# Half of the up projection with seven products, and 29 weight remainders by an adding DMA

## The chip, the cores and the metric

The kernel runs on one core of a Trainium2 chip. The metric is the device time of one execution in microseconds. Matrix products run on TensorE (PE in the profile), elementwise work on VectorE (DVE) and ScalarE (ACT); GpSimd (POOL) and SyncE (SP) mostly issue DMAs here.

## The reference

One layer of an encoder on 256 tokens of width 2048: a retention branch and an attention branch are merged by gates, then comes the MLP, which the change is in. All is float32.

```python
def reference(x, ...):
    h = x
    for l in range(DEPTH):                                # DEPTH = 1
        u = _rmsnorm(h, norm_mix_g[l])
        h = h + _mixer(u, positions, ...)                 # both branches
        z = _rmsnorm(h, norm_mlp_g[l]) @ w_up[l]          # 256x2048 @ 2048x8192
        h = h + jnp.square(jax.nn.relu(z)) @ w_down[l]    # 256x8192 @ 8192x2048
    return _rmsnorm(h, norm_f_g)
```

## The kernel before

**Three products for one.** A float32 operand is split into two parts of the format fp32r: `hi` is a cast of the value, `lo` the remainder value minus `hi`. A product of two operands is then hi·hi + hi·lo + lo·hi. The helper `split` (L548) does it: `SC.copy(hi, val)` on ScalarE, then a subtraction on VectorE. Every weight is loaded as a `raw` tile by a DMA of SP and split before it is used.

**The up projection has two forms.** Of the 64 column tiles of 128, the first `ST` = 24 (`SU` = 3 blocks of 1024 columns) go by seven products instead of eight (class `Step`), and the other 40 go one by one (class `Unit`).

- A `Unit` (L1219) has two parts, one for each half of the 2048 rows of weights. A part loads 512 KB, splits them, and multiplies: `t_pass1` (L176) has eight products of `w.hi` with 512 columns, in which both parts of the tokens lie side by side, `t_pass2` (L180) eight of `w.lo` with 256 columns. Pass 1 needs `hi` alone, pass 2 needs `lo`. After part 1, `evict` copies the bank to `hs` on ScalarE (L1246) and adds its halves on VectorE (L1247). Two iterations later (`later`, `soon`) come relu, square and the store to `hid` in HBM by a DMA of POOL (L1250, L1211, L1212).
- A `Step` has four parts and takes two row tiles of a block, and eight steps (`SJ`) make a block. It forms sums of the weights (L307, L316, L317, on VectorE), splits its seven operands in parts of 2, 2, 2 and 1, and issues 21 products of 512 columns (L333 to L335) with token sums that were made beforehand (`hc`). At a block's end `s_end` (L515) copies four banks on ScalarE and adds on VectorE (L520), and in the next steps four turns (`turn`, L1257) transpose the result on TensorE (L1264), followed by relu, square and store.

**The order is written out by hand.** The list `parts` holds the parts of all units and steps, and behind them those of the down projection. `stream` (L470) goes through it, and all engines keep the order in which it writes their instructions:

```python
for n, (it, h) in enumerate(parts):
    ahead = AHEAD if n else 2                        # AHEAD = 4
    while loaded < min(len(parts), n + ahead + 3): ...   # load of part n+6
    while prepped < min(len(parts), n + ahead + 1): ...  # prep of part n+4
    it.mm(h)                                         # products, and a unit's evict
    after(n)
    soon(n)
```

In ScalarE's queue the preparation of part n+4 thus stands ahead of what `mm` of part n appends, the copy of `evict` among it, and the preparation of part n+5 stands behind it. Tiles come in rings: five for `raw`, and seven pairs for `hi` and `lo`, four of them under these names and three under `morehi` and `morelo`; a pair is free again when TensorE is done with the part seven places before.

**Where the units stand.** The first three units (`EARLY`) go ahead of the steps, the last two (`LATE`) behind them; the turns of the last block are spread over these two. The other 35 stand behind the last part (h = 3) of all 23 steps but the last one, and twelve of them behind the second part (h = 1) of a step.

Of the kernel before, what the change touches and what calls it, by code (L numbers as in the profile page):

```python
# [16 lines left out]
AF = mybir.ActivationFunctionType  # L17
ALU = mybir.AluOpType
# [9 lines left out]
CHUNK = 64  # L28
DFF = 8192
FT = DFF // P  # L30
SU = 3
SJ = KT // 2
ST = SU * 1024 // P
EARLY, LATE = 3, 2
AHEAD = 4
PAIRED = 6
MAKE = 7, 2 * EARLY + 18
SUMS = (4, 7, 10), (0, 1, 2)
MANUAL = {getattr(mybir.EngineType, n) for n in ('Activation', 'DVE', 'PE', 'SP', 'Pool')}
# [66 lines left out]
def block_kernel(ctx: ExitStack, tc: tile.TileContext, A):  # L106
    nc = tc.nc
    V, SC, G, PE = nc.vector, nc.scalar, nc.gpsimd, nc.tensor
# [7 lines left out]
    def big(name, dt=F32, shape=(P, KT, S)):  # L116
        return act.tile(list(shape), dt, tag="act16", name=name)

    class Pair:
        def __init__(self, name):  # L120
            self.t = [big(f"{name}{i}", F32R, (P, KT // 2, 2, S)) for i in range(2)]
# [35 lines left out]
    def wtile(kind, shape):  # L157
        uid[0] += 1
        dt, bufs = (F32, 5) if kind == "raw" else (F32R, 4)
        return wp.tile(shape, dt, tag=kind, bufs=bufs, name=f"{kind}{uid[0]}")  # L160
# [11 lines left out]
    HK = KT // 2  # L172
# [100 lines left out]
    def pair(shape):  # L273
        pool, more = env["pool"], env["more"]
        slot[0] += 1
        if slot[0] % (4 + more) < 4:
            return [wtile(kind, shape) for kind in ("hi", "lo")]
        if env["big"]:
            t = env["big"][:, slot[0] % (4 + more) - 4]
            n = math.prod(shape[1:])  # L280
            return [t[:, i, :n].rearrange("p (a b) -> p a b", a=shape[1]) for i in range(2)]
        return [
            pool.tile(shape, F32R, tag=f"more{kind}", bufs=more, name=f"more{kind}{uid[0]}_{slot[0]}")
            for kind in ("hi", "lo")
        ]

    class Step:
# [17 lines left out]
        def prep(self, part):  # L305
            if part == 0:
                V.tensor_tensor(  # L307
                    out=self.fa, in0=self.rb[:, 1:].to_broadcast([P, 2, 512]), in1=self.ra, op=ALU.add
                )
                self.middle()  # L310
            r = (self.ra, self.fa, self.fb, self.rb[:, :1])[part]
            hi, lo = pair([P, r.shape[1], 512])
            split(hi, lo, r)
            self.ws[part] = hi, lo
            if part == 0:
                V.tensor_tensor(out=self.fb[:, 0], in0=self.fa[:, 0], in1=self.ra[:, 1], op=ALU.add)  # L316
                V.tensor_tensor(out=self.fb[:, 1], in0=self.fb[:, 0], in1=self.rb[:, 0], op=ALU.add)  # L317
# [230 lines left out]
    def split(hi, lo, val, scale=None):  # L548
        if scale is None:
            SC.copy(hi, val)  # L550
            V.tensor_tensor(out=lo, in0=val, in1=hi.bitcast(F32), op=ALU.subtract)  # L551
        else:
            SC.activation(hi, val, AF.Copy, scale=scale)
            V.scalar_tensor_tensor(
                lo, in0=val, scalar=scale, in1=hi.bitcast(F32), op0=ALU.mult, op1=ALU.subtract
            )
# [44 lines left out]
    for k in range(KT):  # L601
        t = lead0[:, N_VEC:] if k == 0 else wtile("raw", [P, LEAD])
# [13 lines left out]
        hi, lo = (wtile(kind, [P, FIRSTS * P]) for kind in ("hi", "lo"))  # L616
# [35 lines left out]
    early = ip.tile([P, FIRSTS, S], F32, name="early")  # L652
# [564 lines left out]
        store(pair, 0, t)  # L1217

    class Unit:  # L1219
        def __init__(self, i, order, between=None):  # L1220
            self.i, self.order, self.between, self.raw, self.ws = i, order, between, {}, {}

        def load(self, part):
            self.raw[part] = wtile("raw", [P, HK, P])
# [1 line left out]

        def prep(self, part):
            hi, lo = pair([P, HK, P])
            split(hi, lo, self.raw.pop(part))
            self.ws[part] = hi, lo  # L1230

        def mm(self, part):
# [24 lines left out]
    def turn(u, jj):  # L1257
        pT = atps(f"zt{u}{jj}")
        for j in range(2):
            kt = 2 * jj + j  # L1260
            for t in range(2):
                o = j * S + t * P
                src = zo[:, 0, 2 * t + kt // 4, kt % 4 * P : kt % 4 * P + P]
                PE.transpose(pT[:, o : o + P], src, ident)  # L1264
        square(4 * u + jj, pT)

    def step(u, j, qs):
        def end():
            sums = s_end(qs, zo[:, 0].rearrange("p (t c) n -> p t c n", t=2), zo[:, 1])
            next(sums)  # L1270
            later.extend([d, lambda: next(sums)] for d in SUMS[u == SU - 1])
            turns.extend(lambda jj=jj: turn(u, jj) for jj in range(4))

        def between():
            if turns and j:
                turns.pop(0)()

        return Step(qs, A["w_up_s"][u, j], hc, j, between, end)

    def drain(n):  # L1280
        def fn(part):
            for _ in range(n[part]):
                turns.pop(0)()
        return fn

    early = [Unit(i, 0) for i in range(EARLY)]
    parts = [(e, h) for h in range(2) for e in early]
    units = list(range(EARLY, FT - ST - LATE))
    slots = [(u, j, h) for u in range(SU) for j in range(SJ) for h in (1, 3)][:-1]
    whole = [t for t in slots if t[2] == 3]  # L1290
    room = len(units) - len(whole)
    halves = [t for t in slots if t[2] == 1]
    if room >= 0:
        use = set(whole) | {halves[i * len(halves) // room] for i in range(room)}
    else:
        use = {t for t in whole if t[1] != PAIRED or t[0] >= -room}
    for u in range(SU):
        qs = {}
        for j in range(SJ):
            st = step(u, j, qs)  # L1300
            for h in range(4):
                parts.append((st, h))
                if (u, j, h) in use:
                    un = Unit(units.pop(0), 0)
                    parts += [(un, 0), (un, 1)]
    assert not units
    for n, i in enumerate(range(FT - ST - LATE, FT - ST)):
        un = Unit(i, 0, drain(((0, 1), (1, 2))[n]))
        parts += [(un, 0), (un, 1)]

    hp = ctx.enter_context(tc.tile_pool(name="hp", bufs=1))
# [57 lines left out]
    def finish(half, t, c, n, lo=0, hi=512):  # L1369
        h = residual(half, t, c)[:, lo:hi]  # L1370
        ps = both[half].q[ROLE[t, c]][:, lo:hi]
        V.scalar_tensor_tensor(h, in0=ps, scalar=rh2[:, t : t + 1], in1=h, op0=ALU.mult, op1=ALU.add)

        def square():
            SC.activation(ps, h, AF.Square, accum_out=ssf[:, t, n : n + 1])

        return square
# [31 lines left out]
    order = [*range(ST // 2, DP), *range(ST // 2)]  # L1409
# [58 lines left out]
    with tc.manual_schedule(engines=MANUAL):  # L1468
        stream(parts, after)
        assert not later  # L1470
        for t in range(2):
            for c in range(2):
# [10 lines left out]
                else:  # L1483
                    halves = [finish(1, t, 1, 3, 0, 256)]
# [86 lines left out]
```

## Time and profile before

| | before |
|---|---|
| time, median of 3 runs | 1578.91 us (1578.73 to 1579.29) |
| profiled execution, first to last instruction (span) | 1577.3 us |
| what lies around the span, median less span | 1.6 us |
| granted TensorE clock, mean | 0.998 |
| busy PE, DVE, ACT, POOL | 1565.2, 1313.6, 959.0, 38.9 us |
| DMA, read from HBM and written to it | 319.72 MB, 12.58 MB |
| up stage | from about 889 to 1236 us of the span |
| down stage | from about 1236 to 1570 us |

The profile gives one execution's span and no time of its own beside it; the span and the median of the runs differ by 1.6 us. Busy times are sums over the instructions of an engine. A matrix product of 512 columns has a duration of about 0.39 us but starts about 0.23 us after the one before, since products overlap; costs on TensorE are therefore read from the starts in the chain of waits, not from the durations.

### The profile page before, as it was taken

To read this page: it belongs to the slowest core of one execution; us is meant where nothing else is said; L and a number is where in the kernel's file an instruction comes from. 1 tells how busy PE (TensorE), PEld (TensorE's weight loads), DVE (VectorE), ACT (ScalarE), POOL (GpSimd) and SP (SyncE) were. 2 spreads that over 40 slices of the span, in tenths; PEclk is the share of its full clock that TensorE was granted. 3 is DMA by queue.
4 is the path that set the end of the run, shared out by engine and by line. 5 is a ranking of instruction groups with operands and counts; after the bars stand their busy time and mean duration, and the time that the engine had idled before them with its cause. 6 is when DMAs were issued, how large, how long until landed. Compare 5 with 4: busy or idle time off the path is not lost.

```text
span 1577.3 us, 21401 instructions
## 1 busy us (share of the span) xinstructions
PE 1565.2 (99%) x7671; PEld 1317.0 (84%) x7671; DVE 1313.6 (83%) x1780; ACT 959.0 (61%) x1405; POOL 38.9 (2%) x75
## 2 busy tenths in 40 slices
PE   9999999999999999999999999999999999999997
PEld 7888888888898888888888888888888888888886
DVE  7898877899967988875667689887978899989996
ACT  6545655566545667765445566676766766666664
POOL 0000000000000000000000000010000100000000
PEclk9999999999999999999999999999999999999999
DMA  8666655466656564443565666667675977786873
GB/s 322 212 197 205 231 164 161 157 203 208 204 178 222 190 203 142 136 135 132 188 214 186 240 221 226 218 209 236 203 246 196 366 267 244 241 308 216 267 254 114
DMA packets 107626, 333.70 MB, mean 212 GB/s; under 512 B 11264, under 2 KB 12160, under 8 KB 106496
## 3 DMA queue, kind: packets, MB, share of 16 engines
q1 hardware_dynamic: 104208, 318.71, 60.5%
q0 software_dynamic: 3168, 11.54, 1.8%
q10 hardware_dynamic: 144, 2.10, 0.4%
q8 instruction: 60, 0.98, 0.3%
q14 instruction: 46, 0.38, 0.1%
HBM read 319.72 MB, written 12.58 MB: 211 GB/s over the span
## 4 chain that ended last, share of the span: by engine, by line
PE 81%; issue 0%; DVE 0%; ACT 0%; DVEq 0%; POOLq 0%; POOL 0%; ACTq 0%
PE z L176 9%; PE dn L357 7%; PE dn L359 7%; PE dn L358 7%; PE z L180 5%; PE zs L333 2%; PE zs L334 2%; PE zs L335 2%; PE lt L199 2%; PE mo L214 2%; PE mo L217 2%; PE mo L215 2%; PE wo L214 2%; PE wo L215 2%; PE wo L217 2%; PE gm L357 2%
## 5 line engine op out<-in xcount | busy, mean ns | idle before, releaser
L169 DVE TENSOR_TENSOR lo<-raw,hi 128x1024 fp32r<-128x1024 f32 (+1 forms) x148 | 173.2, 1172 | 97.2 <-ACT hi L168 97.0
L551 DVE TENSOR_TENSOR lo<-raw,hi 128x1024 fp32r<-128x1024 f32 (+3 forms) x214 | 232.3, 1102 | 22.9 <-ACT hi L550 22.5
L168 ACT CAST hi<-raw 128x1024 fp32r<-128x1024 f32 (+1 forms) x148 | 149.4, 1011 | 166.2 <-PE mo L215 46.2
L550 ACT CAST hi<-raw 128x1024 fp32r<-128x1024 f32 (+3 forms) x214 | 200.1, 954 | 55.5 <-issue 7.8
L551 DVE TENSOR_TENSOR morelo<-raw,morehi 128x1024 fp32r<-128x1024 f32 (+1 forms) x118 | 127.2, 1099 | 19.6 <-ACT morehi L550 19.1
L550 ACT CAST morehi<-raw 128x1024 fp32r<-128x1024 f32 (+1 forms) x118 | 109.1, 950 | 12.6 <-DMA raw<-w_down 3.9
L550 ACT CAST hi<-forms 128x1024 fp32r<-128x1024 f32 x70 | 73.7, 1053 | 51.7 <-DVE forms L307 28.6
L176 PE MATMUL z<-hT,morehi 128*128 128x512 f32 x408 | 101.6, 391 | 0.0
L357 PE MATMUL dn<-hi,dd 128*128 128x512 f32 x230 | 89.7, 390 | 0.0
L359 PE MATMUL dn<-hi,dd 128*128 128x512 f32 x230 | 89.6, 390 | 0.0
L358 PE MATMUL dn<-lo,dd 128*128 128x512 f32 x230 | 89.6, 389 | 0.0
L551 DVE TENSOR_TENSOR lo<-forms,hi 128x1024 fp32r<-128x1024 f32 x70 | 85.0, 1221 | 5.3 <-ACT hi L550 4.9
L176 PEld LDWEIGHTS z<-hT,morehi 128*128 128x128 f32 x408 | 74.9, 188 | 14.4
L1246 ACT COPY hs<-z 128x512 f32<-128x512 f32 x40 | 23.5, 586 | 71.1 <-PE z L180 71.1
L358 PE MATMUL dn<-morelo,dd 128*128 128x512 f32 x156 | 60.8, 390 | 0.0
L357 PE MATMUL dn<-morehi,dd 128*128 128x512 f32 x156 | 60.8, 389 | 0.0
L359 PE MATMUL dn<-morehi,dd 128*128 128x512 f32 x156 | 60.8, 389 | 0.0
L180 PEld LDWEIGHTS z<-hT,morelo 128*128 128x128 f32 x408 | 55.7, 191 | 4.0
L176 PE MATMUL z<-hT,hi 128*128 128x512 f32 x232 | 57.9, 392 | 0.0
L307 DVE TENSOR_TENSOR forms<-raw,sraw 128x1024 f32<-128x1024 f32 x46 | 56.1, 1220 | 1.0 <-DMA raw<-w_up_s 1.0
L180 PE MATMUL z<-hT,morelo 128*128 128x256 f32 x408 | 56.9, 283 | 0.0
L214 PE MATMUL mo<-hi,my 128*128 128x512 f32 x128 | 50.8, 400 | 0.0
(498 smaller groups left out, 4193.8 us busy)
## 6 DMA issues: line engine op xcount, KB each, us to landing
raw<-w_down SPq DMA_DIRECT2D x106, 512.0 KB, 6.1
raw<-w_up SPq DMA_DIRECT2D x80, 512.0 KB, 5.1
raw<-w_rv SPq DMA_DIRECT2D x32, 512.0 KB, 4.8
raw<-w_rg SPq DMA_DIRECT2D x32, 512.0 KB, 4.2
raw<-w_gret SPq DMA_DIRECT2D x32, 512.0 KB, 4.6
raw<-w_ret_o SPq DMA_DIRECT2D x32, 512.0 KB, 5.1
raw<-w_gmla SPq DMA_DIRECT2D x32, 512.0 KB, 4.6
raw<-w_mla_o SPq DMA_DIRECT2D x32, 512.0 KB, 3.7
```

The costliest lines, as they stand in the source:

```text
L168: SC.copy(hi, raw)
L169: V.tensor_tensor(out=lo, in0=raw, in1=hi.bitcast(F32), op=ALU.subtract)
L176: PE.matmul(out, w[0][:, k], x.both(k0 + k), start=start and k == 0, stop=False)
L180: PE.matmul(out[:, :S], w[1][:, k], x.hi(k0 + k), start=False, stop=stop and k == n - 1)
L214: PE.matmul(out, x.hi(k0 + k, ts), w[0][:, k], start=start and k == 0, stop=False)
L215: PE.matmul(out, x.lo(k0 + k, ts), w[0][:, k], start=False, stop=False)
L217: PE.matmul(out, x.hi(k0 + k, ts), w[1][:, k], start=False, stop=stop and k == nk - 1)
L357: PE.matmul(q, ah, wh, start=start, stop=False)
L358: PE.matmul(q, ah, wl, start=False, stop=False)
L359: PE.matmul(q, al, wh, start=False, stop=self.left[f] == 0)
L550: SC.copy(hi, val)
L551: V.tensor_tensor(out=lo, in0=val, in1=hi.bitcast(F32), op=ALU.subtract)
```

## The change

`SU` goes from 3 to 4. Half of the columns of the up projection now go by seven products, and 32 units are left instead of 40: three early, 27 between the steps, two late.

The 27 units stand behind whole steps alone: there are 31 such places (the last step's is left out), and `use` spreads the units over them evenly, so that four places stay empty. `PAIRED` and the places in the middle of a step are gone.

All units but the three early ones (27 + 2 = 29) get `added=True`. In part 0 of such a unit the remainder is not subtracted on VectorE. ScalarE casts the weights to `hi` as before and casts them once more with the scale -1 into `lo`, which then holds -hi; then POOL issues a DMA that reads the same 512 KB of weights from HBM again and adds them to `lo`. Part 1 of the unit, the early units and the steps are split as before.

```diff
-SU = 3
+SU = 4
...
-PAIRED = 6
...
     class Unit:
-        def __init__(self, i, order, between=None):
-            self.i, self.order, self.between, self.raw, self.ws = i, order, between, {}, {}
+        def __init__(self, i, added=True, between=None):
+            self.i, self.added, self.between, self.raw, self.ws = i, added, between, {}, {}
...
         def prep(self, part):
             hi, lo = pair([P, HK, P])
-            split(hi, lo, self.raw.pop(part))
+            raw = self.raw.pop(part)
+            if part == 0 and self.added:
+                SC.copy(hi, raw)
+                SC.activation(lo, raw, AF.Copy, scale=-1.0)
+                G.dma_start(lo, A["w_up"][self.i][:, part * HK : (part + 1) * HK], accum_op=ALU.add)
+            else:
+                split(hi, lo, raw)
             self.ws[part] = hi, lo
...
-    early = [Unit(i, 0) for i in range(EARLY)]
+    early = [Unit(i, False) for i in range(EARLY)]
     parts = [(e, h) for h in range(2) for e in early]
     units = list(range(EARLY, FT - ST - LATE))
-    slots = [(u, j, h) for u in range(SU) for j in range(SJ) for h in (1, 3)][:-1]
-    whole = [t for t in slots if t[2] == 3]
-    room = len(units) - len(whole)
-    halves = [t for t in slots if t[2] == 1]
-    if room >= 0:
-        use = set(whole) | {halves[i * len(halves) // room] for i in range(room)}
-    else:
-        use = {t for t in whole if t[1] != PAIRED or t[0] >= -room}
+    whole = [(u, j, 3) for u in range(SU) for j in range(SJ)][:-1]
+    use = {whole[i * len(whole) // len(units)] for i in range(len(units))}
...
                 if (u, j, h) in use:
-                    un = Unit(units.pop(0), 0)
+                    un = Unit(units.pop(0))
                     parts += [(un, 0), (un, 1)]
...
-        un = Unit(i, 0, drain(((0, 1), (1, 2))[n]))
+        un = Unit(i, True, drain(((0, 1), (1, 2))[n]))
         parts += [(un, 0), (un, 1)]
```

## The prediction

> **What bounds the kernel now.** I read the chain that ended last first, then the up stage alone (from 889 to 1236 us of the span) in the windows, then who waits for whom inside it.
>
> ```profile
> PE 81%; issue 0%; DVE 0%; ACT 0%; DVEq 0%; POOLq 0%; POOL 0%; ACTq 0%
> ```
>
> ```profile
> core 0: us, PE busy (x) PEld busy (x) DVE busy (x) ACT busy (x) POOL busy (x), PEclk, DMA share, GB/s
> 889.00:1236.00 347.00, 346.99 (x1852) 299.11 (x1851) 292.53 (x335) 237.22 (x340) 26.10 (x48) 1.00 0.67 225
> ```
>
> ```profile
> ACT hs L1246 <- PE z L180: 71.1, 38, 3.6
> ...
> PEld zs L335 <- DVE lo L551: 0.4, 1, 0.4
> ```
>
> The chain is made of matrix products. In the up stage TensorE (PE) is busy 346.99 of 347.00 us at a granted clock of 1.00, VectorE (DVE) 292.53, ScalarE (ACT) 237.22. TensorE waited for a weight once, for 0.4 us. ScalarE waited 71.1 us in 38 places, always in the same one: the copy that empties a unit's bank stands in ScalarE's queue and holds it until the unit's last product is done. So in this stage a product less is time less, as long as every remainder `lo` is there when TensorE asks for it, and the wait in ScalarE's queue decides how early ScalarE can begin with the next one.
>
> **What seven products save.** The chain, in order of time, shows a unit and a step side by side.
>
> ```profile
> 1078.44 1.81 PE z L176 x8
> 1080.25 0.95 PE z L180 x8
> 1081.20 1.84 PE z L176 x8
> 1083.05 0.95 PE z L180 x8
> 1084.00 0.23 PE zs L333
> ...
> 1088.79 1.81 PE z L176 x8
> ```
>
> ```profile
> L1264 PE MATMUL zt<-con,zo 128*128 128x128 f32 x48 | 7.0, 272 | 0.0
> ```
>
> A unit of 128 columns takes 1.81 + 0.95 + 1.84 + 0.95 = 5.55 us, a step of 21 products 88.79 - 84.00 = 4.79 us. The change takes out eight units (44.4 us) and puts in eight steps (38.3 us) and four turns of four transposes each (16/48 of 7.0 us, 2.3 us). TensorE's work falls by 44.4 - 40.6 = 3.8 us. That is all there is to win: 0.24% of the time.
>
> **What it costs VectorE and ScalarE.** The groups of the up stage give the prices.
>
> ```profile
> L551 DVE TENSOR_TENSOR lo<-forms,hi 128x1024 fp32r<-128x1024 f32 x48 | 58.1, 1221 | 4.9 <-ACT hi L550 4.9
> L307 DVE TENSOR_TENSOR forms<-raw,sraw 128x1024 f32<-128x1024 f32 x24 | 29.3, 1219 | 1.0 <-DMA raw<-w_up_s 1.0
> L1247 DVE TENSOR_TENSOR hs<-hs 128x256 f32<-128x256 f32 x40 | 17.0, 424 | 27.6 <-ACT hs L1246 26.6
> L317 DVE TENSOR_TENSOR forms<-forms,raw 128x512 f32<-128x512 f32 x24 | 16.6, 692 | 0.8
> L316 DVE TENSOR_TENSOR forms<-forms,sraw 128x512 f32<-128x512 f32 x24 | 16.5, 686 | 0.0
> L520 DVE TENSOR_TENSOR zo<-zo 128x512 f32<-128x512 f32 x12 | 8.1, 684 | 0.0
> L520 DVE TENSOR_TENSOR zo<-zs,zo 128x512 f32<-128x512 f32 x9 | 6.2, 688 | 0.2
> ```
>
> ```profile
> L550 ACT CAST hi<-forms 128x1024 fp32r<-128x1024 f32 x48 | 50.5, 1053 | 26.1 <-DVE forms L307 18.3 <-DVE forms L317 7.8
> L1246 ACT COPY hs<-z 128x512 f32<-128x512 f32 x40 | 23.5, 586 | 71.1 <-PE z L180 71.1
> L1211 ACT ACTIVATE hs<-hs 128x256 f32<-128x256 f32 (+1 forms) x49 | 22.9, 467 | 1.6
> L1250 ACT ACTIVATE hs<-hs 128x256 f32<-128x256 f32 x38 | 15.6, 411 | 4.8 <-DVE hs L1247 4.7
> L1216 ACT ACTIVATE hs<-zt 128x512 f32<-128x512 f32 x12 | 7.2, 597 | 0.5 <-PE zt L1264 0.5
> L522 ACT COPY zo<-zs 128x512 f32<-128x512 f32 x3 | 1.7, 575 | 0.0
> ```
>
> VectorE: a step is one form of 1.22, two of 0.69, three remainders of 1.22 and one of half that size, for which I take the 0.69 of the other half-size operations, 6.95 us in all; eight are 55.6, and the sums at the end of a block are a third of 8.1 + 6.2, 4.8. Out go eight units with two remainders of 1.2 and one addition of 0.42 each (22.6), and 29 remainders (34.8). The balance is +3.0 us: 295 us of work beside some 343 us of TensorE. ScalarE: eight steps of 3 x 1.05 and a half-size cast of 0.6 (30.0), four copies of 0.58 and four turns with an activation and a square of about 0.6 each (7.1), less eight units with two casts of 1.05, a copy of 0.59, 0.41 and 0.47 (28.6). To that come 29 negated casts, an operation that the trace does not have; as one pass over 128x1024 it is nearest to the cast's 1.05 us, so 30.5. The balance is +39 us, 276 of 343. Neither becomes the bound by its sum; both are hidden behind TensorE. What is not hidden is the order.
>
> **Where the new DMA stands.** At iteration n of the stream ScalarE's queue gets the preparation of part n+4 first and the unit's copy after it. With units only behind whole steps, the order is four step parts, then a unit's two parts. The copy at a unit's end therefore stands in the queue ahead of the cast for the first part of the next unit, and only four step parts lie between them on TensorE. The trace of before has that very pattern between 1084 and 1094 us: ScalarE's, POOL's and TensorE's timeline.
>
> ```profile
> 1084.04 0.59 ACT L1246 COPY hs<-z 128x512 f32<-128x512 f32 x1 [1.38 <-PE z L180]
> 1084.52 2.00 ACT L550 CAST morehi<-raw 128x1024 fp32r<-128x1024 f32 x2
> ...
> 1086.86 0.42 ACT L1211 ACTIVATE hs<-hs 128x256 f32<-128x256 f32 x1
> ```
>
> ```profile
> 1087.58 0.54 POOL L1212 DMA_DIRECT2D hid<-hs  x1 [6.30 <-ACT hs L1211]
> ```
>
> ```profile
> 1088.62 1.98 PE L176 MATMUL z<-hT,morehi 128*128 128x512 f32 x8
> 1090.43 1.12 PE L180 MATMUL z<-hT,morelo 128*128 128x256 f32 x8
> ```
>
> The copy waits for TensorE and starts at 1084.04; the two casts of the next unit follow at once. In the changed kernel the second cast's place is taken by the negated cast of part 0, which then ends at 1084.52 + 2.00 = 1086.52. POOL began its store 0.30 us after ScalarE's end (1087.58 against 1086.86 + 0.42), so the adding DMA is issued at 1086.82. TensorE takes the unit's first pass, on `hi` alone, at 1088.62 and asks for `lo` at 1090.43. The budget from issue to landing is 3.6 us. Before, one subtraction of 1.2 us lay there, and 2.4 us were to spare.
>
> What does the adding DMA of 512 KB take? It is not in the trace; the rows around it, all of the up stage, are these (the last is of the loads into `raw`):
>
> ```profile
> raw<-w_up SPq DMA_DIRECT2D x74, 512.0 KB, 5.4
> sraw<-w_up_s SPq DMA_DIRECT2D x23, 512.0 KB, 7.4
> ...
> hid<-hs POOLq DMA_DIRECT2D x38, 128.0 KB, 4.4
> ...
> hid<-hs POOLq DMA_DIRECT2D x10, 256.0 KB, 5.8
> ```
>
> ```profile
> DMA to landing us min/median/max: 3.5/5.4/10.0
> ```
>
> Below: the fastest plain load of the same size took 3.5 us, and an adding DMA also reads what it adds to. Above: the slowest took 10.0. From POOL's own stores, 4.4 at 128 KB and 5.8 at 256 KB, a straight line gives 8.6 at 512 KB. I take 7.4, the row of the same size, direction and stage that shares its time with other loads: the load that refills the freed `raw` buffer goes out at the same moment. The stall is 7.4 - 3.6 = 3.8 us.
>
> The Trainium skill (DMA: Bandwidth & Descriptors, "Anatomy of one DMA") says that a DMA from the GpSimd queue costs about 2.0 us and its bytes at 436 GB/s. By that the 512 KB would land in an estimated 3.2 us and nothing would stall. The trace disagrees for its own 128 KB stores: the rule gives 2.3 us, the row 4.4.
>
> How often? With four blocks there are 31 places behind whole steps (the last left out) and 27 units to spread over them, so places 7, 15, 23 and 30 stay empty. In 23 cases the preceding copy is a unit's, in the first that of the last early unit; in the three behind an empty place at a block's end four copies of 0.58 stand there instead of one, 1.7 us more each. All 27 are gated. The two late units follow a step without a unit, so their preparation is held by no copy just before, and I count nothing for them; if that cover fails, it is two stalls more. Twelve of the 27 have a turn's four transposes (7.0/12 = 0.58 us) among the four step parts, which lengthens their budget. Sum: 27 x 3.8 + 3 x 1.7 - 12 x 0.58 = 102.6 + 5.1 - 7.0 = 100.7 us. Behind the stalled unit nothing is late next: ScalarE waits at the unit's copy, VectorE has caught up, and the next unit begins the same wait anew. POOL's queue holds only a store behind each adding DMA, which nobody awaits soon.
>
> Together: -3.8 + 100.7 = +96.9 us. The profiled execution's span is 1577.3 us, which gives 1674; the median of the runs, 1578.91, lies 1.6 us above that span, and with the same 1.6 us the forecast is 1676 us. A measurement of this kernel can tell about 0.2% (3 us) from no change.
>
> **The rivals.** *It lands in time.* If the adding DMA lands within 3.6 us of its issue, the stalls are gone and the 3.8 us remain: 1575 us, faster. For it: the fastest plain load, 3.5. Against it: that is the lowest of the loads, with a median of 5.4, and this one has more to do. It decides at 3.6 us. I give it 0.07, and 0.05 to landings between 3.6 and 4.4 us, which end between 1575 and 1595 us.
>
> *The clock falls in the stalls.* In before TensorE is never idle in this stage, and the granted clock is 1.00 in the windows row above; no row shows what it does after a pause of some 4 us. If it halved until the unit's end, the three passes behind the stall (0.95 + 1.84 + 0.95 = 3.7 us) would take 3.7 us more, 100 us over 27 units and 1776 us; with half of the stalls hit, 1726 us. I give that 0.12. The Trainium skill (TensorE: Matmul & The Clock Gate, "HAM oscillation — how this bites in real kernels") has such a rule against this change: a pause of over about 3.4 us halves the clock. No row here bears on it, since TensorE never pauses.
>
> *The adding DMA is much slower than a load*, over 10.0 us: at 10.0 the sum is 27 x 6.4 - 1.9 - 3.8 = +167, 1746 us, and it grows by 27 us with each further microsecond. For it: it reads twice, and the DMA engines' share is 0.67 already. Against it: while TensorE waits they have less to do. 0.08.
>
> **How the numbers follow.** The forecast, landings between 4.4 and 10.0 us at full clock, has 0.68. The range runs from 1595 us (a stall of 0.8 us: 21.6 - 1.9 - 3.8 = +16) to 1770 us, most of the way into the case of the falling clock; the cases of timely landing and of landings far over 10 us are left out, together some 0.18. Faster has 0.07, no change 0.02 from the near misses, slower 0.91.
>
> **What would show it.** In the changed profile TensorE's weight loads of `z<-hT,lo` at L180's place wait for the DMA into `lo` some 27 times, 3 to 5 us each, and the DMA issues list `lo<-w_up` 29 times on POOL's queue with a median over 4.4 us. A unit's first pass over `hi` begins on time, and the pause lies between the two passes of part 0, never in part 1. VectorE's busy time in the stage stays within some 5 us of 292.5 and ScalarE's rises by about 39. I am wrong if ScalarE issues that negated cast a unit's length earlier than the copy allows, if the landing is under 3.6 us, or if the pauses lie before `hi`.

## The result, and the profile after

The changed kernel takes 1763.2 us (median of 4 runs, 1761.42 to 1767.0) against 1578.91 us before; the ratio is 1.117, with a 95% interval of 1.1154 to 1.1185. The profiled execution has a span of 1759.4 us, 182.1 us more than before. In the chain that ended last the share of TensorE has fallen from 81% to 59%, and the DMA into the remainders stands in it by name.

```profile
PE 59%; issue 17%; DMA 4%; POOL 1%; DVE 1%; ACT 1%; POOLq 0%; DVEq 0%; ACTq 0%
PE dn L356 6%; PE dn L358 6%; PE dn L357 6%; DMA lo<-w_up 2%; PE lt L198 2%; PE z L175 2%; DMA morelo<-w_up 2%; PE z L179 2%; PE mo L213 2%; PE mo L216 2%; PE mo L214 2%; PE wo L213 2%; PE wo L214 2%; PE wo L216 2%; PE gm L358 2%
```

The up stage (889 to 1420 us, where it used to end at 1236) in the windows; the columns are as before, span, busy time of PE, PEld, DVE, ACT and POOL, the granted clock, the DMA share and GB/s:

```profile
889.00:1420.00 531.00, 404.39 (x1788) 333.44 (x1788) 296.74 (x345) 275.09 (x377) 51.41 (x75) 0.87 0.62 177
```

VectorE has 296.74 us of work there and ScalarE 275.09: neither is near its limit. TensorE is idle for 531.00 - 404.39 = 126.6 us, and its busy time has grown to 404.39 us although the change takes 3.8 us of products away. Its own waits, over the same stretch:

```profile
PE z L179 <- DMA lo<-w_up: 62.6, 15, 6.4
PE z L179 <- DMA morelo<-w_up: 56.4, 13, 6.9
PE zs L332 <- ACT zo L521: 6.1, 3, 2.0
PE zs L332 <- DVE zo L519: 1.6, 3, 0.5
```

The first two rows are the adding DMA: 28 pauses, 119.0 us, 4.25 us each. The other two are 7.7 us of another kind, at the ends of blocks. Together they are the idle time. The rest is the clock, 0.87 instead of 1.00 in the windows row. To compare like with like, the stage has to end at the first product of the down stage, at 1234.77 us before and at 1416.88 us after: to there TensorE is busy 345.8 and 401.3 us, so the products that are left take 401.3 - (345.8 - 3.8) = 59.3 us longer. (The 61 us in the expectations below are this term read from the two windows rows; the later one holds 1.9 us more of the down stage.) The balance of the stage is 126.6 + 59.3 - 3.8 = 182.1 us, just what the span is longer.

One unit in close-up, from the timelines of ScalarE, POOL and TensorE; the numbers are start, duration, and in brackets the idle time before:

```profile
1195.29 0.59 ACT L1251 COPY hs<-z 128x512 f32<-128x512 f32 x1 [6.69 <-PE z L179]
1195.78 1.05 ACT L1230 CAST hi<-raw 128x1024 fp32r<-128x1024 f32 x1
1196.72 1.06 ACT L1231 ACTIVATE lo<-raw 128x1024 fp32r<-128x1024 f32 x1
```

```profile
1198.17 0.89 POOL L1232 DMA_DIRECT2D lo<-w_up  x1 [13.88 <-ACT lo L1231]
```

```profile
1200.36 1.97 PE L175 MATMUL z<-hT,hi 128*128 128x512 f32 x8
1205.72 1.21 PE L179 MATMUL z<-hT,lo 128*128 128x256 f32 x8 [3.40 <-DMA lo<-w_up]
1206.77 3.38 PE L175 MATMUL z<-hT,hi 128*128 128x512 f32 x8
1209.94 1.34 PE L179 MATMUL z<-hT,lo 128*128 128x256 f32 x8
```

ScalarE idles for 6.69 us at the copy, and casts only then. POOL issues the DMA 0.39 us after the negated cast's end (1196.72 + 1.06). Pass 1 on `hi` starts without a wait, and pass 2 waits 3.40 us for `lo`. Then the eight products of pass 1 in part 1 take 3.38 us where the row of before, in the prediction, has 1.98. That is the lower clock, after the pause: between 1206.80 and 1209.90 us the granted clock is 0.54, and in the pass before the pause, between 1200.40 and 1202.20 us, it is 1.00.

The landings of the two tile names, from the DMA issues (count, size, median):

```profile
lo<-w_up POOLq DMA_DIRECT2D x16, 512.0 KB, 7.9
morelo<-w_up POOLq DMA_DIRECT2D x13, 512.0 KB, 7.9
```

### The profile page after: what moved, and what is told of

Same layout as the page of the kernel before. It is cut to its first block, busy times and chain, and to the rows that moved or that the text cites. A ratio compares the mean times of both kernels' runs of the same rounds, so it can differ in the third digit from the quotient of the medians.

```text
span 1759.4 us, 21396 instructions
## 1 busy us (share of the span) xinstructions
PE 1620.6 (92%) x7599; PEld 1349.6 (77%) x7599; DVE 1317.6 (75%) x1790; ACT 995.3 (57%) x1438; POOL 63.1 (4%) x100
## 4 chain that ended last, share of the span: by engine, by line
PE 59%; issue 17%; DMA 4%; POOL 1%; DVE 1%; ACT 1%; POOLq 0%; DVEq 0%; ACTq 0%
PE dn L356 6%; PE dn L358 6%; PE dn L357 6%; DMA lo<-w_up 2%; PE lt L198 2%; PE z L175 2%; DMA morelo<-w_up 2%; PE z L179 2%; PE mo L213 2%; PE mo L216 2%; PE mo L214 2%; PE wo L213 2%; PE wo L214 2%; PE wo L216 2%; PE gm L358 2%
## 5 line engine op out<-in xcount | busy, mean ns | idle before, releaser
L1251 ACT COPY hs<-z 128x512 f32<-128x512 f32 x32 | 18.8, 587 | 183.4 <-PE z L179 183.4
L179 PE MATMUL z<-hT,lo 128*128 128x256 f32 x296 | 52.1, 328 | 62.6 <-DMA lo<-w_up 62.6
L179 PEld LDWEIGHTS z<-hT,lo 128*128 128x128 f32 x296 | 48.7, 233 | 71.7 <-DMA lo<-w_up 68.9
L550 DVE TENSOR_TENSOR morelo<-raw,morehi 128x1024 fp32r<-128x1024 f32 (+1 forms) x75 | 78.4, 1057 | 31.6 <-ACT morehi L549 31.5
L175 PE MATMUL z<-hT,hi 128*128 128x512 f32 x296 | 94.5, 473 | 0.0
L179 PE MATMUL z<-hT,morelo 128*128 128x256 f32 x216 | 40.5, 343 | 56.4 <-DMA morelo<-w_up 56.4
L179 PEld LDWEIGHTS z<-hT,morelo 128*128 128x128 f32 x216 | 37.5, 247 | 63.7 <-DMA morelo<-w_up 61.8
L549 ACT CAST morehi<-forms 128x1024 fp32r<-128x1024 f32 x50 | 52.5, 1050 | 55.2 <-DVE forms L316 33.0
L175 PEld LDWEIGHTS z<-hT,hi 128*128 128x128 f32 x296 | 68.9, 240 | 14.8
L549 ACT CAST morehi<-raw 128x1024 fp32r<-128x1024 f32 (+1 forms) x75 | 67.9, 914 | 6.5 <-issue 2.1
L175 PE MATMUL z<-hT,morehi 128*128 128x512 f32 x216 | 67.5, 466 | 0.0
```

The lines of the kernel that those rows point to most:

```text
L175: PE.matmul(out, w[0][:, k], x.both(k0 + k), start=start and k == 0, stop=False)
L179: PE.matmul(out[:, :S], w[1][:, k], x.hi(k0 + k), start=False, stop=stop and k == n - 1)
```

## The experiments

Theory W says: the adding DMA is issued too late because its casts stand behind the preceding unit's copy, TensorE waits, and the clock falls in the pauses. Rival S puts the time on the seven products and the new places of the units, rival D on the DMA itself, its bytes and descriptors, wherever it stands.

**Seven products alone.** All units subtract on VectorE again.

```diff
-                    un = Unit(units.pop(0))
+                    un = Unit(units.pop(0), False)
...
-        un = Unit(i, True, drain(((0, 1), (1, 2))[n]))
+        un = Unit(i, False, drain(((0, 1), (1, 2))[n]))
```

> The changed kernel with the remainders of all units subtracted on VectorE again; four blocks by seven products and the new places of the units stay. Theory W (the wait for the adding DMA behind the unit's copy, and the clock that falls in that wait): no weight load waits for a DMA, the clock is back at 1.00 and the time is near before, 1575 to 1590 us; VectorE gets some 38 us more in the stage than before, 330 of some 343 us, so a few microseconds of waits for it are possible. Rival S (seven products in four blocks, or the new places of the units, cost the time): it stays above 1650 us.

Measured: 1586.67 us (1584.59 to 1587.48, five runs), ratio to before 1.0046 (1.0033 to 1.0058). S falls: of 184 us no more than 8 are left. But the half of the change that saves work is by itself slower than before. Its TensorE waits, from 889 to 1240 us, tell why:

```profile
PE zs L332 <- ACT zo L521: 6.4, 3, 2.4
PE zs L332 <- DVE zo L519: 1.6, 3, 0.5
PE zs L334 <- DVE morelo L550: 0.8, 1, 0.8
```

Eight of the 8.8 us lie at three ends of blocks. The even spread leaves places 7, 15 and 23 empty, and each of them is the last step of a block: no unit stands between two blocks, and the next block needs the banks that ScalarE and VectorE are still reading. In before a unit stood there, and in the same stage TensorE has no wait of this kind.

**The adding DMA alone**, in the kernel before (three blocks, 37 units with `added`, units behind half steps too).

```diff
 SU = 3
...
-            split(hi, lo, self.raw.pop(part))
+            raw = self.raw.pop(part)
+            if part == 0 and self.added:
+                SC.copy(hi, raw)
+                SC.activation(lo, raw, AF.Copy, scale=-1.0)
+                G.dma_start(lo, A["w_up"][self.i][:, part * HK : (part + 1) * HK], accum_op=ALU.add)
+            else:
+                split(hi, lo, raw)
```

> The kernel before with the adding DMA alone: three blocks, 37 units with an added remainder in part 0. Theory W with numbers of the trace after (4.25 us of wait where four step parts lie between copy and unit): 12 units have only two parts of 2.75 us between and 12 only 2.06 us, so their waits are 6.3 and 7.0 us, 11 have 4.25, together some 206 us; with 2.2 us of slow products for each, some 77 us, the time is about 1860 us (1820 to 1900), slower than the whole change. Rival S: near before, under 1600 us. If the DMA's bandwidth were the cost and not its place, 37 against 29 DMAs would give 1763 + 8/29 of 184, about 1814 us.

Measured: 1701.41 us, one run, a span of 1699.3 us. The DMA does the harm without the fourth block, but my number was 160 us too high. I had counted a wait for each of 35 units:

```profile
PE z L180 <- DMA morelo<-w_up: 80.3, 23, 6.5
PE z L180 <- DMA lo<-w_up: 0.7, 1, 0.7
```

There were 24, and those in `lo` are as good as free. ScalarE's timeline of this run shows where one of these stands:

```profile
1082.24 1.04 ACT L550 CAST hi<-forms 128x1024 fp32r<-128x1024 f32 x1
1083.19 1.04 ACT L1231 CAST hi<-raw 128x1024 fp32r<-128x1024 f32 x1
1084.14 1.05 ACT L1232 ACTIVATE lo<-raw 128x1024 fp32r<-128x1024 f32 x1
```

The preceding unit's second pass over part 0 only begins at 1087.57, so these casts are ahead of its copy and not behind it. With two step parts between two units, n+4 reaches past the copy. I had shortened the budget and forgotten that the wait in the queue goes away. The 25 DMAs into `morelo` waited 23 times, the 12 into `lo` once, and landings were alike (8.3 and 8.5 us): the place decides, not the DMA. The 12 in `lo` are the units behind the first half of a step. The 11 units with four step parts before them waited 4.2 us on average, as I had counted. But 11 of the 12 units behind the second half of a split step waited too, 2.7 us on average, though their casts stand ahead of the preceding copy as well. Their budget is still shorter than a landing: behind the first half of a step, an addition issued at 1050.96 is asked for at 1060.20 (9.2 us, no wait), and the next one, behind the second half, is issued at 1061.07 and asked for at 1067.99 (6.9 us, a wait of 2.45 us).

**One part earlier.** In the up and down stages part n+5 is prepared before part n's copy.

```diff
-        while prepped < min(len(parts), n + ahead + 1):
+        while prepped < min(len(parts), n + ahead + 1 + more):     # more = 1
```

> The changed kernel, with the preparation in the up and down stages written one part earlier, so that the casts and the adding DMA of a unit stand ahead of the preceding unit's copy in ScalarE's queue. Loads stay where they are. Theory W: ScalarE issues them while it used to idle for that copy, 3 to 4 us earlier, so a landing of 7.9 us meets a budget of about 7: waits fall from 4.25 to under 1.5 us, the clock stays near 1.00, 1575 to 1620 us. Rival D (the adding DMA's load on the DMA engines or POOL's descriptors slow the stage, wherever it stands): over 1700 us.

Measured: 1644.21 us (1642.5 to 1650.02), ratio 1.0418 (1.04 to 1.0436): two thirds of the loss are gone by order alone, but it is 24 us above my range. TensorE's waits from 889 to 1300 us:

```profile
PE z L179 <- DMA morelo<-w_up: 23.4, 8, 5.2
PE z L179 <- DMA lo<-w_up: 18.4, 10, 2.7
PE zs L332 <- ACT zo L521: 4.8, 3, 2.0
```

Eighteen waits of 2.3 us are left, and the products are still 21 us slower than at full clock. Landings grew from 7.9 to 9.6 and 9.5 us, which takes back some 1.6 us of the budget gained, while the DMA share rose from 0.62 to 0.79. That a shorter stage moves the same bytes in less time would be rival D's part in this. It is likely, but not shown: three adding DMAs alone, in a run below, land as late at a share of 0.70.

**Products in the pauses.** The first pass of part 0 runs three times, so TensorE has 29 x 16 products more.

```diff
             t_pass1(self.ps, w, hT, part * HK, HK, part == 0)
+            if part == 0 and self.added:
+                t_pass1(self.ps, w, hT, 0, HK, False)
+                t_pass1(self.ps, w, hT, 0, HK, False)
```

> The changed kernel with 16 more products of 512 columns (first pass of part 0 twice more, so those units' sums hold the hi product three times) between pass 1 and pass 2 of every unit with an added remainder: 29 x 3.65 us = 106 us more work for TensorE, put into the pauses. Theory W with the clock as its second half: pauses fall from 4.25 to some 0.6 us, the granted clock returns to near 1.00 and the 61 us that the same products took longer are gone; with 4 us for the late unit that has no pause, about 1706 us (1695 to 1725), faster with more work. Rival C (the products are slow for another reason than the pauses, a shared port or the DMA's traffic): 1763 us or more.

Measured: 1722.29 us (1720.42 to 1726.76), ratio to before 1.0902 (1.0885 to 1.0919), inside the range. The kernel does 106 us more products than the change and is 41 us faster.

```profile
889.00:1380.00 491.00, 461.67 (x2218) 381.84 (x2217) 294.79 (x343) 270.39 (x368) 49.65 (x72) 0.98 0.66 191
```

The clock is back at 0.98, and pauses for the DMA are 22.5 us instead of 119.0. The window ends 2.5 us before the stage does. Up to the first product of the down stage, at 1382.48, TensorE is busy 464.1 us, and 106 of them are the added products; 358.1 are left where the change has 401.3, so 43 of the 59 us of slow products have gone with the pauses. Rival C, slow products for another reason than pauses, falls: the DMA share is no lower than in the change (0.66 against 0.62).

**The DMA in part 1.**

```diff
-            if part == 0 and self.added:
+            if part == 1 and self.added:
```

> The changed kernel with the adding DMA moved from part 0 to part 1 of the same 29 units. In ScalarE's queue the negated cast then stands one cast later (0.95 us), but TensorE asks for that remainder 2.76 us later, so the budget grows by 1.8 us. Theory W: waits of 4.25 - 1.8 = 2.4 us, 65 us over 27 units, far less slow product time (10 to 20 us instead of 61), and the 8 us at the ends of blocks as in the run with seven products alone: about 1663 us (1640 to 1685). Rival D (the DMA's load or POOL): unchanged at 1763 us, since bytes, DMAs and instructions are the same.

Measured: 1672.17 us (1669.83 to 1673.04), ratio 1.0584 (1.0568 to 1.06), inside the range.

```profile
PE z L179 <- DMA lo<-w_up: 35.4, 16, 4.2
PE z L179 <- DMA morelo<-w_up: 23.9, 11, 5.4
```

Twenty-seven waits of 2.2 us with a landing of 8.1 us: the same DMAs, bytes and casts, placed where TensorE asks later, cost 91 us less. The waits sum to 59 us instead of 65; the slow products cost 31 us and not 10 to 20, so that part of my sum was too low.

**A plain copy instead of the addition** (`lo` is then the weight itself).

```diff
-                G.dma_start(lo, A["w_up"][self.i][:, part * HK : (part + 1) * HK], accum_op=ALU.add)
+                G.dma_start(lo, A["w_up"][self.i][:, part * HK : (part + 1) * HK])
```

> The changed kernel with the DMA into lo copying the weights instead of adding them (lo is then the weight itself). What does the adding cost? If reading lo back and adding is what makes the landing 7.9 us, a plain copy lands near the plain loads' 5 us, waits fall from 4.25 to about 1.4 us, and the time to about 1630 us. If the place and the load of the DMA engines make the landing, it stays near 7.9 us and 1760 us.

Measured: 1675.5 us, one run. Neither number was met; it lies between the two. The issues of this run:

```profile
raw<-w_up SPq DMA_DIRECT2D x58, 512.0 KB, 4.4
...
lo<-w_up POOLq DMA_DIRECT2D x16, 512.0 KB, 6.2
morelo<-w_up POOLq DMA_DIRECT2D x13, 512.0 KB, 5.7
```

From POOL the plain 512 KB take 6.0 us, 1.6 us more than the same weights take from SP, and the adding DMA of the changed kernel takes another 1.9 us. Not even a DMA that adds nothing would meet the budget at that place.

**The empty places moved**, seven products alone.

```diff
-    use = {whole[i * len(whole) // len(units)] for i in range(len(units))}
+    use = {t for t in whole if t[1] != 3}
```

> Seven products alone, no adding DMA, with the four empty places moved from the ends of blocks (7, 15, 23) and place 30 to the fourth step of every block. In the run with seven products alone TensorE waited some 8 to 10 us at the three ends of blocks, for ScalarE's and VectorE's reading of the block's banks, since no unit stood between two blocks. Theory P (the places cause it): these waits vanish and the time falls from 1586.7 to about 1578 us (1574 to 1582). Rival V (VectorE, with 321 of 347 us busy, has not the time, wherever the units stand): 1584 us or more, with waits for lo in their place.

Measured: 1580.0 us (1579.37 to 1582.27, 11 runs), ratio 1.0007 (0.9998 to 1.0016). The waits at the ends of blocks are gone and with them 6.7 us; three waits for VectorE's subtractions in the first block, 4.9 us, are what is left. P holds, and V holds for those three.

**Part 1, two parts earlier, places moved.** This is the 29 DMAs at the best place that I found.

```diff
-            if part == 0 and self.added:
+            if part == 1 and self.added:
...
-        while prepped < min(len(parts), n + ahead + 1):
+        while prepped < min(len(parts), n + ahead + 1 + more):     # more = 2
...
-    use = {whole[i * len(whole) // len(units)] for i in range(len(units))}
+    use = {t for t in whole if t[1] != 3}
```

> An attempt at a version of the change that pays: adding DMA in part 1, preparations written two parts earlier, so that the negated cast stands ahead of the preceding unit's copy, and the empty places away from the ends of blocks. Theory W: a budget of about 9 to 10 us against landings of 8 to 9.6 us leaves few waits; VectorE is at some 295 of 343 us: 1574 to 1590 us. Rival D: over 1620 us, since the same bytes are moved in less time and landings grow as in the run with one part earlier (9.5 us).

Measured: 1593.35 us (1592.71 to 1595.84), ratio 1.0089 (1.0075 to 1.0103), 3 us above my range. TensorE's eight waits for the DMA sum to 11.6 us, landings are 9.0 and 9.4 us, the DMA share is 0.87. The DMA now costs little, but it does not pay: the same places and the same order without any adding DMA take 1582.36 us (the last run below), 11 us less.

**Three more, to end.** Seven products alone (all units `False`) with the moved places and preparations one part earlier:

```diff
+    use = {t for t in whole if t[1] != 3}
...
+        while prepped < min(len(parts), n + ahead + 1 + more):     # more = 1
```

> Seven products alone with the empty places in the fourth steps, and the preparations written one part earlier. In the run without the earlier preparation TensorE waited three times, 5 to 6 us in all, for a subtraction on VectorE in the first block. If these waits come of preparations that begin too late behind a unit's copy, they shrink and the time falls from 1580.0 to about 1575 us (1573 to 1578), below before; if VectorE has no time there at all (the sums of the tokens are made in the same stretch), it stays at 1580 us.

Measured: 1576.63 us (1575.99 to 1578.23, 11 runs), ratio 0.9981 (0.9972 to 0.999). Three waits became two of 1.1 us in all. It is the one run below before, by 0.19%, and it has no adding DMA. The interval of the ratio lies below 1, but the gain is about as small as the 3 us that the prediction calls the least to be told from no change. The last two have the moved places, preparations two parts earlier (`more = 2`), and differ only in three adding DMAs in part 1, behind the first three steps:

```diff
-                    un = Unit(units.pop(0), False)
+                    un = Unit(units.pop(0), u == 0 and j < 3)
```

> The same places, preparations two parts earlier, and the adding DMA (in part 1) for only three units, those behind the first three steps, where VectorE was late. Theory W: three landings of 9 us against a budget of 9 to 10 us and VectorE 3.6 us freer in that stretch: waits of under 2 us in all, 1574 to 1578 us, below before. Rival: any adding DMA in that stretch waits as in the change, 3 x 4 us more, 1585 us or more.

> The same as the run with three adding DMAs, without any: seven products, empty places in the fourth steps, preparations two parts earlier. It tells what the three DMAs give: if VectorE's time in the first block is the limit, this one is 3 to 5 us slower than that run; if the order is, both are alike at about 1575 us.

Measured: 1582.41 us (1581.54 to 1584.76), ratio 1.002 (1.0012 to 1.0029), with the three DMAs, and 1582.36 us (1581.99 to 1583.71), ratio 1.0018 (1.0009 to 1.0027), without. Both expectations failed. With the three DMAs TensorE waits 3.2 us for one of them; without them it waits 3.3 us in four places of the up stage, 1.1 us of that for VectorE. So the DMAs gave nothing. Two parts earlier is slower than one by some 6 us. Both runs show waits for ScalarE that the run with one part earlier has not: for its reading of a turned bank (0.4 us with the DMAs, 1.3 us without) and, in the down stage, 1.1 us more. That is less than 6 us, and no run shows where the rest comes from.

## Why the prediction was right, and where it was short

The side, the place and the wait for the adding DMA were right, and 1763.2 us lies in the range. But my likeliest time was 1676 us, 87 us too low: 59.3 us of that are the clock, which I took to be full, 18.3 us the pauses and 7.7 us the ends of blocks. The other 2 us are that the profiled execution, on which these terms are read, was the fastest of the four. The range reached 1763.2 us only because I had stretched it into the case of the falling clock, to which I gave 0.12; at full clock my sum ended at 1746 us with the slowest landing. So that the range holds is in part luck. Point by point:

- **Work saved and added.** VectorE 296.74 us (predicted 295), ScalarE 275.09 (276), and neither bound the stage. The negated cast, priced at 1.05 us, took 1.06.
- **Budget and landing.** I expected 3.6 us and 7.4 us, a stall of 3.8 us. The landing was 7.9, POOL began 0.39 us after the cast and not 0.30, and the pause was 4.25 us on average (2.81 to 6.43 us for the 27). The first rival, in time, falls: the fastest landing was 5.8 us. Its supporting rule in the Trainium skill (DMA: Bandwidth & Descriptors, "Anatomy of one DMA") gave 3.2 us. The measured 7.9 us decides against it for the adding DMA, and the 6.0 us of the plain copy from POOL do too.
- **Count.** 28 pauses instead of 27: the first of the two late units waited as well, 6.91 us, the failure of the cover that I had named. No copy held its casts, as I had said, but the last step's own preparations did: they began at 1391.49, 6.15 us after the copy before them. In all 119.0 us instead of 100.7.
- **Ends of blocks.** I let the empty places there lengthen a unit's wait, by 5.1 us in all, but missed that TensorE itself waits for the banks: 7.7 us. The term was left out of the sum, and the run with moved places shows what it is. The 5.1 us themselves do not show: the three units concerned waited 3.91, 4.20 and 4.15 us, no longer than the rest.
- **The clock.** This step failed. I gave the falling clock 0.12, priced half of it at 50 us and all at 100, and left it out of the forecast since no row of before shows a pause. It fell and cost 59.3 us, 2.1 us for each pause. With it at my price of 50 the sum would have been 1726 us. That 50 is near 59 is luck, though: slow products followed 26 of the 28 pauses and not half of them, and cost some 2.3 us each time and not 3.7.

What I could have seen is that the stall I forecast, 3.8 us, was itself longer than the pause of about 3.4 us named by the rule quoted in the prediction. The Trainium skill (TensorE: Matmul & The Clock Gate, "HAM oscillation — how this bites in real kernels") agrees with the runs in direction: from 3.65 us on every pause of the changed kernel was followed by slow products. Pauses under that length are not safe, though. These are TensorE's timelines, first the change, then the run with the plain copy:

```profile
1082.32 1.22 PE L179 MATMUL z<-hT,morelo 128*128 128x256 f32 x8 [3.42 <-DMA morelo<-w_up]
1083.37 2.00 PE L175 MATMUL z<-hT,morehi 128*128 128x512 f32 x8
```

```profile
1283.15 1.21 PE L179 MATMUL z<-hT,morelo 128*128 128x256 f32 x8 [1.79 <-DMA morelo<-w_up]
1284.20 3.42 PE L175 MATMUL z<-hT,morehi 128*128 128x512 f32 x8
```

After 3.42 us of pause the next eight products of pass 1 took 2.00 us, at a granted clock of 1.00; after only 1.79 us, in the other kernel, they took 3.42, at 0.52. A pause below the rule's length can cost the clock, and one as long can escape it.

## What to carry to other kernels

Before work is moved to a DMA, follow it through the queue of the engine that starts it: what stands ahead there, when that is let go, and when the consumer asks. Here the budget was 3.6 us against a landing of 7.9, while ScalarE, which makes what the DMA adds to, idled some 6 us at a copy one place ahead (183.4 us in 30 places); the busy shares showed nothing of it. Price every forecast pause of TensorE with its clock as well, and when work is spread evenly over places, look at which places stay empty.

## What the runs showed of the hardware

A pause of TensorE can cost more than its length: in some cases 1.3 to 2.9 us of slow products follow a pause of 1.8 to 3.4 us, in others none, and 1.4 to 2.8 us followed every one of 3.65 us or more in the changed kernel. Here TensorE was better off with useless products than with pauses: 106 us of them made the kernel 41 us faster.

A DMA of 512 KB from HBM into on-chip memory took 4.4 us from SP and 6.0 us from POOL in the same stage, and 7.9 us from POOL with an addition; 29 of these at a higher DMA share (0.79 to 0.87) took 9.0 to 9.6 us, but three alone, in the first block and at a share of 0.70, took 9.0 and 9.4 us as well, so the stage's share is not all that sets the landing. POOL's instruction itself took 0.89 us when adding, against 0.54 us for the plain copy.
